# Loads moved to ScalarE's queue, five steps ahead, and the seeds of the last product moved up

## The chip, the cores and the metric

The kernel runs on one core of a Trainium2 chip. The core has five engines with instruction queues of their own: TensorE (PE, with its weight loads shown as PEld), VectorE (DVE), ScalarE (ACT), GpSimd (POOL) and SyncE (SP). SP, POOL and ACT can also issue DMA transfers, which sixteen DMA engines carry out. An engine takes its queue in order: an instruction that waits holds up all behind it. The metric is the device time of one execution in microseconds, the median over the runs of the kernel.

## The reference

One encoder layer on x of 1024 rows and 2048 columns, in float32:

```python
h = rmsnorm(x, pre_g) * (1.0 + scale) + shift            # scale, shift, gate from silu(c) @ w_ada + b_ada
q, k, v, gate_a, u, gate_p = jnp.split(h @ w_in, SPLIT_POINTS, axis=-1)
y_a = windowed_gqa(q, k, v, rel_table, sink) * silu(gate_a)   # window 128, relative bias, sink
y_p = multiscale_pool(u, w_pool_grp, pool_scale) * silu(gate_p)
g_a, g_p = jnp.split(sigmoid(h @ w_merge + b_merge), 2, axis=-1)
merged = g_a * (y_a @ w_branch_attn) + g_p * (y_p @ w_branch_pool)
return x + gate * rmsnorm(merged @ w_out, post_g)
```

## The kernel before, in words

**Products.** A float32 operand is split into a high and a low part (`split`, lines 90 to 92: ACT writes the high part, DVE subtracts for the low one), and a product is hi x hi, hi x lo and lo x hi. The large products run by a Strassen scheme with seven products instead of eight for each 2 x 2 of blocks, named B11, T3, T2, B21, T4, T1, B22. For `h @ [w_in, w_merge]` (`strassen`, line 198) the weights come in 34 pairs of 128 columns. A pair is seven products of 12 matmuls, one after another, into banks called X, Z and V. Its weights are loaded by SP (`raw`), summed by DVE, split by ACT and DVE into a ring of four (`whi`, `wlo`), and the banks are evicted by ACT. The inner dimension is taken in two halves: a first pass over all 34 pairs with the first 1024 columns of h (partial sums go to `part_d`), and a second pass with the others.

**Side work.** While PE multiplies, `run` (line 309) calls one step of a queue `side` at given points of each pair; with `every` of (0, 1, 3, 4, 6) these are five steps a pair. `placed` puts a step's PE and DVE instructions behind the last matmul and the last low-part split issued so far (`tc.issue_after`). Apart from such edges a planner sets the order on every engine: it takes the instructions that are ready by its own cost model's times, those written first going first, so work may be issued earlier than it is written, and a wait that lasts longer on the chip than in the model holds up what stands behind it.

**Bias lines** (`bias_lines`, line 594) run in the first pass as one side step: a small product gives one line of 512 relative-bias values per head; ACT evicts it, POOL stores it to `line_d` and then copies it 128 times for each of 8 heads into `bias_d` (2 MB, DRAM to DRAM), which attention reads much later.

**The x stage** (lines 687 to 752) is made of the last ten pairs of the first pass, 50 side steps. It builds the second half of h, transposed. `fetch_x` loads a tile of 128 x 512 of x through POOL's queue (`side_load`) and scales it on ACT; three steps later `turn_x` transposes it with four matmuls, and ACT copies the result into H. There are sixteen tiles, in a ring of four (`xt2`). Sixteen steps of `modulate` and four of `pre_op` follow. Into these steps `with_sums` hangs eight of the sixteen weight sums for the output product: `weight_sums` (line 628) loads four tiles of `w_out` through POOL into a ring of four of their own (`ws2`), DVE makes four sums three steps later, and POOL stores them to `ws_d`. They start at steps 2, 6, ..., 30. In the last pair, the planned operand of the second pass begins to be split (`refill`, line 741), and more of it follows in the first pair of the second pass.

**The end.** The output product runs in four blocks of seven products of 48 matmuls. `load_wo` fetches the weights of a product, `prep_wo` splits them, `product` (line 1109) multiplies and calls `prep_wo` for the next one. In the last block (lines 1319 to 1355) T4, T1 and B22 go row by row (`by_rows`), so that bank t is done after a quarter of the product. `squares` sums a result's squares on ACT, `weigh` multiplies it by the gate row on DVE, and `finish_rows` closes a row of 128 x 2048: the norm's factor, four operations on DVE (line 1316) and four stores by SP. B22 accumulates on top of seeds: DVE adds `last["12"]` to the banks that hold T1's result, after these were weighed. Before the change the four rows of the first half are closed in one loop behind T4, and the seeds of B22 follow behind T1.

Of the kernel before, what the change touches and what calls it, by code (L numbers as in the profile page):

```python
# [20 lines left out]
P = 128  # L21
# [21 lines left out]
def encoder_layer(ctx: ExitStack, tc: tile.TileContext, x, c, table, w_ada, b_ada, pre_g,  # L43
# [27 lines left out]
    dram = ctx.enter_context(tc.tile_pool(name="dram", bufs=1, space=DRAM))  # L71
    psum = ctx.enter_context(tc.tile_pool(name="psum", bufs=4, space=PSUM))

    cnt, pairs_, last_mm, last_lo = [0], [0], [None], [None]

    def uid(s):
        cnt[0] += 1
        return f"{s}_{cnt[0]}"

    def bank(tag, name="b"):  # L80
        return psum.tile([P, 512], F32, tag=tag, name=uid(name), bufs=1 if tag in SEEDED else 2)
# [6 lines left out]


    def split(hi, lo, src):  # L90
        nc.scalar.activation(hi, src, AF.Copy)  # L91
        return nc.vector.tensor_tensor(lo, src, f32(hi), ALU.subtract)  # L92

    def placed(f):
# [6 lines left out]
    def add(o, a, b, eng=None):  # L101
        (eng or nc.vector).tensor_tensor(o, a, b, ALU.add)  # L102
# [467 lines left out]
    def pass1(n, side, every=(0, 2, 4, 6), then=None):  # L570
        nonlocal i
        for m in range(n):
            w, n0 = weight_of(ORDER[i])
            run(strassen(w, n0, 0, range(4), op, to_dram(block(part_d, ORDER[i]))),
                side, every, None, then if m == n - 1 else None)
            i += 1
# [17 lines left out]
    def bias_lines():  # L594

        nc.gpsimd.memset(tab, 1.0)
        side_load(tab[0:32, :], table)
        oh = ev.tile([P, 512], F32, tag="ev", name="oh")[0:33, :]
        side_load(oh, onehot)
        pb = bank("sc")  # L600
        nc.tensor.matmul(pb[0:NH, :], tab, oh, start=True, stop=True)
        bl = ev.tile([P, 512], F32, tag="ev", name="bl")[0:NH, :]
        nc.scalar.activation(bl, pb[0:NH, :], AF.Copy)
        side_store(line_d, bl)
        side_store(bias_d.rearrange("h (p l) -> h p l", l=LINE),
              bass.AP(line_d.tensor, line_d.offset, [[LINE, NH], [0, P], [1, LINE]]))

    grow = gp.tile([KT, 4, P], F32, name="grow")
# [39 lines left out]
    def with_sums(steps, first, stride, ns, tile_):  # L648

        got = {}  # L650

        def begin(f, n):
            got[n] = weight_sums(n, tile_)
            f()

        def end(f, n):
            f()
            got.pop(n)()

        for i_, n in enumerate(ns):  # L660
            a, b = first + i_ * stride, first + i_ * stride + 3
            steps[a] = lambda f=steps[a], n=n: begin(f, n)
            steps[b] = lambda f=steps[b], n=n: end(f, n)
        return steps
# [25 lines left out]
    h = {HALF + k: [H[s][:, k] for s in range(2)] for k in range(HALF)}  # L690

    def x_tile():
        return sp.tile([P, 512], F32, tag="xt2", name=uid("xt"), bufs=4)

    def sum_tile():
        return sp.tile([P, 512], F32, tag="ws2", name=uid("wsum"), bufs=4)

    def fetch_x(si, q):
        xt = x_tile()
        c0 = 1024 + q * 512  # L700
        side_load(xt, x[si * P:(si + 1) * P, c0:c0 + 512])
        nc.scalar.activation(xt, xt, AF.Copy, scale=rstd[:, si:si + 1])
        return xt

    def turn_x(si, q, xt):
        pt = bank("sc")
        for j in range(4):
            nc.tensor.transpose(pt[:, j * P:(j + 1) * P], xt[:, j * P:(j + 1) * P], ident)
        nc.scalar.activation(H[si // 4][:, 4 * q:4 * q + 4, (si % 4) * P:(si % 4 + 1) * P],
                             pt.rearrange("p (k t) -> p k t", k=4), AF.Copy)  # L710

    held = {}

    def x_step(n):
        if n < 2 * NB:
            held[n] = fetch_x(n // 2, n % 2)
        if n >= 3:
            turn_x((n - 3) // 2, (n - 3) % 2, held.pop(n - 3))

    steps = [lambda n=n: x_step(n) for n in range(2 * NB + 3)]  # L720
    steps += [lambda k=k, s=s: modulate((nc.scalar, nc.vector)[s], h[k][s], k) for k in h for s in range(2)]
    side = deque(with_sums(steps, 2, 4, range(8, 16), sum_tile))
    h1, h2 = ({j: h[HALF + ktile(kh, j)] for j in range(4)} for kh in range(2))
    t2 = {}

    def pre(j):
        t2[j] = pre_op(j, h1, h2, x_tile)

    side.extend(lambda j=j: pre(j) for j in range(4))

    def put_all(o, name, h1, h2, t2):
        for j in range(4):
# [13 lines left out]
                                                             3: part_of("T1"), 5: part_of("B22")}  # L746

    op2, ahead, before, among = refill(h1, h2, t2)
    pass1(PAIRS - i, side, (0, 1, 3, 4, 6), ahead)
    assert not side  # L750
    all_of(before)
    op = op2
# [353 lines left out]
            ws.append((hi, lo))  # L1106
        ready.append(ws)

    def product(mov, banks, fresh, by_rows=False):
        ws = ready.popleft()  # L1110
        load_wo()
        order = [(t, j) for t in range(4) for j in range(KS)] if by_rows else \
            [(t, j) for j in range(KS) for t in range(4)]
        for t, j in order:
            hi, lo = op[mov][j]
            wh, wl = ws[j]
            ts_ = slice(t * P, (t + 1) * P)
            for n, (m_, w_) in enumerate(((hi, wh), (hi, wl), (lo, wh))):
                nc.tensor.matmul(banks[t], m_[:, ts_], w_, start=fresh and j == 0 and n == 0,  # L1119
                                 stop=j == KS - 1 and n == 2, skip_group_check=True)  # L1120
        prep_wo()

    def four(tag, bufs=4):
        return [ev.tile([P, 512], F32, tag=tag, name=uid(tag), bufs=bufs) for _ in range(4)]
# [177 lines left out]
    def fetch_rows(half, t):  # L1302
        si = half * 4 + t
        rows_x[si] = [slot("xr", F32) for _ in range(4)]
        for n in range(4):
            side_load(rows_x[si][n], x[si * P:(si + 1) * P, n * 512:(n + 1) * 512])

    def finish_rows(half, t):
        si = half * 4 + t
        s_ = const.tile([P, 4], F32, tag="st", name=uid("st"), bufs=2)  # L1310
        nc.vector.tensor_reduce(s_[:, 0:1], ssq[:, si], op=ALU.add, axis=AX.X)
        nc.scalar.activation(s_[:, 1:2], s_[:, 0:1], AF.Sqrt, bias=eps_t, scale=1.0 / D)
        nc.vector.reciprocal(s_[:, 2:3], s_[:, 1:2])
        for n in (1, 3, 2, 0):
            o_ = (last, kept)[n % 2][f"{n // 2 + 1}{half + 1}"][t]
            nc.vector.scalar_tensor_tensor(o_, o_, s_[:, 2:3], rows_x[si][n], op0=ALU.mult, op1=ALU.add)  # L1316
            store(out[si * P:(si + 1) * P, n * 512:(n + 1) * 512], o_)

    bx, bz = new_banks(3)
# [7 lines left out]
    for t in range(2):  # L1327
        fetch_rows(0, t)
    product("T3", bz, False)
    for t in range(4):  # L1330
        add(bx[t], bz[t], last["21"][t])
    for t in range(4):
# [1 line left out]
        sub(last["12"][t], last["12"][t], bz[t])  # L1334
    for t in range(2, 4):
        fetch_rows(0, t)
    product("T4", bx, False, by_rows=True)
    for t in range(2):
        fetch_rows(1, t)
    for t in range(4):  # L1340
        squares(0, "21", t, bx[t])
        weigh(0, "21", last["21"][t], bx[t])
        finish_rows(0, t)
    product("T1", bz, False, by_rows=True)
    for t in range(2, 4):
        fetch_rows(1, t)
    for t in range(4):
        squares(0, "22", t, bz[t])
        weigh(0, "22", last["22"][t], bz[t])
        add(bz[t], bz[t], last["12"][t])  # L1350
    product("B22", bz, False, by_rows=True)
    for t in range(4):
        squares(0, "12", t, bz[t])
# [40 lines left out]
```

## Time and profile before

| | |
|---|---|
| median of 3 runs | 2172.62 us (2171.68 to 2174.97) |
| profiled execution, its own time | 2174.68 us |
| its span, first to last instruction | 2172.8 us |
| mean granted clock of PE | 0.988 |
| PE busy | 2101.9 us, 97% |
| DVE busy | 1501.2 us, 69% |
| ACT busy | 1081.7 us, 50% |
| POOL busy | 187.7 us, 9% |
| first pass, x stage: loads of x issued | 555.4 to 635.1 us |
| last block: first matmul of B22 | 2147.98 us |

A line of the profile's timeline gives the start, the duration, the engine, the line of the kernel, the operation with the tile written and those read, the count, and in brackets the idle time of the engine before it and what ended it. Instructions that only issue a DMA are shown on SPq, ACTq or POOL. A line of the waits gives the total, the count and the longest. Matmuls are pipelined: PE shows 0.39 us for one of 512 columns, and the next one starts 0.23 us later.

### The profile page before, as it was taken

What the parts mean: (1) busy time and instruction counts of PE and PEld (TensorE: products, weight loads), DVE (VectorE), ACT (ScalarE), POOL (GpSimd) and SP (SyncE); (2) the same over time, 40 slices, a digit from 0 to 9 for tenths busy, and PEclk for the clock granted to TensorE, in tenths of its full rate; (3) what the DMA queues carried; (4) which work ended last, traced back from release to release, by engine and by line L of the source; (5) the groups of instructions that cost most, each with busy time, mean ns of one, the idle gap of its engine ahead of it and who ended that gap; (6) DMA issues with size and microseconds to landing.
All of it is one profiled execution on the core that took longest, in us unless ns stands there. A gap on an engine that the chain in (4) does not pass through costs nothing.

```text
span 2172.8 us, 29010 instructions
## 1 busy us (share of the span) xinstructions
PE 2101.9 (97%) x9638; PEld 1725.6 (79%) x9638; DVE 1501.2 (69%) x2695; ACT 1081.7 (50%) x2006; POOL 187.7 (9%) x407
## 2 busy tenths in 40 slices
PE   5999999889989999999999999999999999999997
PEld 3688788668878888888888888888788888788885
DVE  6688556777446686767776777866967987655558
ACT  6664444234364464576667433333645655545342
POOL 0402102431232000000000000000000000000021
PEclk9999999999999999999999999999999999999998
DMA  9768645997567446455554576675654646776367
GB/s 329 263 228 300 210 154 201 333 325 235 184 222 243 137 151 206 160 168 170 182 173 140 190 225 217 214 236 170 231 168 162 213 138 205 253 262 227 98 213 252
DMA packets 267430, 455.63 MB, mean 210 GB/s; under 512 B 24154, under 2 KB 120562, under 8 KB 267280
## 3 DMA queue, kind: packets, MB, share of 16 engines
q1 hardware_dynamic: 238048, 359.21, 50.5%
q0 software_dynamic: 28896, 94.51, 12.8%
q8 instruction: 76, 1.25, 0.2%
q14 instruction: 74, 0.61, 0.1%
q10 hardware_dynamic: 336, 0.06, 0.0%
HBM read 321.53 MB, written 134.24 MB: 210 GB/s over the span
## 4 chain that ended last, share of the span: by engine, by line
PE 78%; DMA 12%; DVE 6%; issue 2%; ACT 1%; POOL 1%; SPq 0%; DVEq 0%; ACTq 0%; POOLq 0%
PE Z L222 26%; PE V L222 18%; PE X L222 18%; PE OUT L1119 11%; DMA ada<-in_w_ada_dram 2%; DMA gada<-in_w_ada_dram 2%; DMA xt<-in_x_dram 1%; DMA raw<-in_w_merge_dram 1%; DVE wlo L92 1%; DMA raw<-in_w_in_dram 1%; DVE po L1316 1%; DMA gt<-proj_d 1%; PE PT L851 1%; DMA lm<-m_d 1%; PE GEMV L432 1%
## 5 line engine op out<-in xcount | busy, mean ns | idle before, releaser
L91 ACT ACTIVATE whi<-raw 128x512 fp32r<-128x512 f32 (+1 forms) x540 | 321.2, 600 | 512.6 <-PE Z L222 247.1
L92 DVE TENSOR_TENSOR wlo<-raw,whi 128x512 fp32r<-128x512 f32 (+1 forms) x540 | 347.6, 650 | 166.5 <-PE Z L222 107.1
L102 DVE TENSOR_TENSOR raw<-raw,raw 128x512 f32<-128x512 f32 x78 | 53.8, 690 | 122.9 <-DMA raw<-in_w_merge_dram 73.0
L92 DVE TENSOR_TENSOR wlo<-wr,whi 128x512 fp32r<-128x512 f32 x112 | 76.2, 687 | 76.9 <-ACT whi L91 74.9
L91 ACT ACTIVATE whi<-wr 128x512 fp32r<-128x512 f32 x112 | 69.3, 627 | 100.1 <-PE OUT L1119 98.2
L222 PE MATMUL X<-B11h,whi 128*128 128x512 f32 x336 | 94.3, 399 | 7.9 <-ACT c L292 5.4
L222 PE MATMUL V<-T3h,whi 128*128 128x512 f32 x336 | 93.4, 396 | 8.5 <-DVE u L102 7.8
L222 PE MATMUL V<-T4h,wlo 128*128 128x512 f32 x336 | 91.9, 393 | 1.9 <-DVE wlo L92 1.9
L222 PE MATMUL X<-B11l,whi 128*128 128x512 f32 x336 | 93.2, 396 | 0.4 <-DVE B11l L92 0.4
L222 PE MATMUL V<-T4h,whi 128*128 128x512 f32 x336 | 92.9, 395 | 0.5 <-ACT T4h L91 0.5
L222 PE MATMUL Z<-T2h,whi 128*128 128x512 f32 x336 | 91.9, 392 | 1.4 <-ACT Z L248 1.4
L222 PE MATMUL Z<-T2h,wlo 128*128 128x512 f32 x336 | 91.8, 392 | 1.4 <-DVE wlo L92 1.4
L222 PE MATMUL Z<-T1h,whi 128*128 128x512 f32 x336 | 92.4, 392 | 0.8 <-ACT T1h L91 0.7
L222 PE MATMUL X<-B11h,wlo 128*128 128x512 f32 x336 | 93.2, 397 | 0.0
L222 PE MATMUL Z<-B22h,whi 128*128 128x512 f32 x336 | 92.1, 393 | 0.6 <-ACT u L271 0.6
L222 PE MATMUL V<-T3l,whi 128*128 128x512 f32 x336 | 92.4, 394 | 0.0
L222 PE MATMUL V<-T3h,wlo 128*128 128x512 f32 x336 | 92.2, 394 | 0.0
L222 PE MATMUL X<-B21h,wlo 128*128 128x512 f32 x336 | 91.1, 390 | 1.1 <-DVE wlo L92 1.1
L222 PE MATMUL X<-B21h,whi 128*128 128x512 f32 x336 | 92.0, 392 | 0.0
L222 PE MATMUL V<-T4l,whi 128*128 128x512 f32 x336 | 91.9, 393 | 0.0
L222 PE MATMUL Z<-T2l,whi 128*128 128x512 f32 x336 | 91.5, 391 | 0.0
L222 PE MATMUL Z<-B22h,wlo 128*128 128x512 f32 x336 | 91.1, 390 | 0.0
(361 smaller groups left out, 5041.9 us busy)
## 6 DMA issues: line engine op xcount, KB each, us to landing
part<-part_d SPq DMA_DIRECT2D x136, 256.0 KB, 4.8
raw<-in_w_merge_dram SPq DMA_DIRECT2D x64, 512.0 KB, 5.5
raw<-in_w_in_dram SPq DMA_DIRECT2D x60, 512.0 KB, 4.1
ada<-in_w_ada_dram POOLq DMA_DIRECT2D x96, 256.0 KB, 6.0
proj_d<-part SPq DMA_DIRECT2D x68, 256.0 KB, 2.2
wsum<-in_w_out_dram POOLq DMA_DIRECT2D x64, 256.0 KB, 6.2
ws_d<-wsum POOLq DMA_DIRECT2D x64, 256.0 KB, 4.9
gada<-in_w_ada_dram POOLq DMA_DIRECT2D x32, 512.0 KB, 6.5
```

What stands on the lines that cost most here:

```text
L91: nc.scalar.activation(hi, src, AF.Copy)
L92: return nc.vector.tensor_tensor(lo, src, f32(hi), ALU.subtract)
L102: (eng or nc.vector).tensor_tensor(o, a, b, ALU.add)
L222: last_mm[0] = nc.tensor.matmul(ps, w_[:, i], op[mov][j][m_], start=fresh and i == 0 and n == 0, stop=i == nj - 1 and n == 2, skip_group_c ...
L432: nc.tensor.matmul(pv[g][r:r + 32, :], scz[:, kc, :], tiles[kc][:, g], start=b == 0, stop=b == 3, tile_position=(0, r))
L851: nc.tensor.transpose(pt[:, i * P:(i + 1) * P], p[:, i * P:(i + 1) * P], ident)
L1119: nc.tensor.matmul(banks[t], m_[:, ts_], w_, start=fresh and j == 0 and n == 0, stop=j == KS - 1 and n == 2, skip_group_check=True)
L1316: nc.vector.scalar_tensor_tensor(o_, o_, s_[:, 2:3], rows_x[si][n], op0=ALU.mult, op1=ALU.add)
```

## The change

1. The broadcast of the bias lines into `bias_d` is issued by ACT instead of POOL; the small store before it stays on POOL.
2. The loads of x in the x stage are issued by ACT. The ring `xt2` has eight tiles and serves the weight sums too (`ws2` is gone; the memory is the same). A tile is turned five steps after its load, not three. The scaling on ACT moves from the load to the turn and is put behind the newest high-part split (`last_hi`).
3. The stage's eight weight sums start at steps 17, 21, ..., 45 instead of 2, 6, ..., 30, and the queue of steps is filled up to 50 with empty ones.
4. In the last block, T1's weights are split behind T3 (an extra `prep_wo`), and T4 splits none; B22's weights are split behind the closing of rows 0 and 1 of the first half (on DVE, behind its last operation, `last_lo`). Row 2 is closed behind T1's matmuls, and row 3 behind the seed of B22's first bank.

```diff
     def split(hi, lo, src):
-        nc.scalar.activation(hi, src, AF.Copy)
+        last_hi[0] = nc.scalar.activation(hi, src, AF.Copy)
         return nc.vector.tensor_tensor(lo, src, f32(hi), ALU.subtract)
...
-        side_store(bias_d.rearrange("h (p l) -> h p l", l=LINE),
+        nc.scalar.dma_start(bias_d.rearrange("h (p l) -> h p l", l=LINE),
...
     def x_tile():
-        return sp.tile([P, 512], F32, tag="xt2", name=uid("xt"), bufs=4)
-
-    def sum_tile():
-        return sp.tile([P, 512], F32, tag="ws2", name=uid("wsum"), bufs=4)
+        return sp.tile([P, 512], F32, tag="xt2", name=uid("xt"), bufs=8)
 
     def fetch_x(si, q):
         xt = x_tile()
         c0 = 1024 + q * 512
-        side_load(xt, x[si * P:(si + 1) * P, c0:c0 + 512])
-        nc.scalar.activation(xt, xt, AF.Copy, scale=rstd[:, si:si + 1])
+        nc.scalar.dma_start(xt, x[si * P:(si + 1) * P, c0:c0 + 512])
         return xt
 
     def turn_x(si, q, xt):
+        with tc.issue_after(last_hi[0].ins):
+            nc.scalar.activation(xt, xt, AF.Copy, scale=rstd[:, si:si + 1])
         pt = bank("sc")
...
-    held = {}
+    held, AHEAD = {}, 5
...
-        if n >= 3:
-            turn_x((n - 3) // 2, (n - 3) % 2, held.pop(n - 3))
+        if n >= AHEAD:
+            turn_x((n - AHEAD) // 2, n % 2 ^ AHEAD % 2, held.pop(n - AHEAD))
...
-    side = deque(with_sums(steps, 2, 4, range(8, 16), sum_tile))
...
-    side.extend(lambda j=j: pre(j) for j in range(4))
+    steps += [lambda j=j: pre(j) for j in range(4)]
+    every = (0, 1, 3, 4, 6)
+    steps += [lambda: None] * (len(every) * (PAIRS - i) - len(steps))
+    side = deque(with_sums(steps, 2 * NB + 1, 4, range(8, 16), x_tile))
...
-            nc.vector.scalar_tensor_tensor(o_, o_, s_[:, 2:3], rows_x[si][n], op0=ALU.mult, op1=ALU.add)
+            last_lo[0] = nc.vector.scalar_tensor_tensor(o_, o_, s_[:, 2:3], rows_x[si][n],
+                                                        op0=ALU.mult, op1=ALU.add)
...
     product("T3", bz, False)
+    prep_wo()
...
-    product("T4", bx, False, by_rows=True)
+    product("T4", bx, False, by_rows=True, prepare=False)
     for t in range(2):
         fetch_rows(1, t)
-    for t in range(4):
+
+    def close_rows(t):
         squares(0, "21", t, bx[t])
         weigh(0, "21", last["21"][t], bx[t])
         finish_rows(0, t)
+
+    for t in range(2):
+        close_rows(t)
+    with tc.issue_after(last_lo[0].ins):
+        prep_wo()
     product("T1", bz, False, by_rows=True)
     for t in range(2, 4):
         fetch_rows(1, t)
+    close_rows(2)
     for t in range(4):
         squares(0, "22", t, bz[t])
         weigh(0, "22", last["22"][t], bz[t])
         add(bz[t], bz[t], last["12"][t])
+        if t == 0:
+            close_rows(3)
```

More of the change, by code (lines that the diff above doesn't have):

```diff
@@ L72, in encoder_layer @@
     psum = ctx.enter_context(tc.tile_pool(name="psum", bufs=4, space=PSUM))
-    cnt, pairs_, last_mm, last_lo = [0], [0], [None], [None]
+    cnt, pairs_, last_mm, last_lo, last_hi = [0], [0], [None], [None], [None]
     def uid(s):
@@ L716, in x_step @@
             held[n] = fetch_x(n // 2, n % 2)
-        if n >= 3:
-            turn_x((n - 3) // 2, (n - 3) % 2, held.pop(n - 3))
-    steps = [lambda n=n: x_step(n) for n in range(2 * NB + 3)]
+        if n >= AHEAD:
+            turn_x((n - AHEAD) // 2, n % 2 ^ AHEAD % 2, held.pop(n - AHEAD))
+    steps = [lambda n=n: x_step(n) for n in range(2 * NB + AHEAD)]
     steps += [lambda k=k, s=s: modulate((nc.scalar, nc.vector)[s], h[k][s], k) for k in h for s in range(2)]
-    side = deque(with_sums(steps, 2, 4, range(8, 16), sum_tile))
     h1, h2 = ({j: h[HALF + ktile(kh, j)] for j in range(4)} for kh in range(2))
@@ L748, in encoder_layer @@
     op2, ahead, before, among = refill(h1, h2, t2)
-    pass1(PAIRS - i, side, (0, 1, 3, 4, 6), ahead)
+    pass1(PAIRS - i, side, every, ahead)
     assert not side
@@ L1107, in prep_wo, with product @@
         ready.append(ws)
-    def product(mov, banks, fresh, by_rows=False):
+    def product(mov, banks, fresh, by_rows=False, prepare=True):
         ws = ready.popleft()
@@ L1120, in product @@
                                  stop=j == KS - 1 and n == 2, skip_group_check=True)
-        prep_wo()
+        if prepare:
+            prep_wo()
     def four(tag, bufs=4):
@@ L1343, in encoder_layer @@
         finish_rows(0, t)
+    for t in range(2):
+        close_rows(t)
+    with tc.issue_after(last_lo[0].ins):
+        prep_wo()
     product("T1", bz, False, by_rows=True)
```

## The prediction

> **What bounds the kernel now.** I read the page first, then the busy time of the engines over stretches of 50 us to find where TensorE (PE) idles, then those places in order of time.
>
> ```profile
> span 2172.8 us, 29010 instructions
> PE 2101.9 (97%) x9638; PEld 1725.6 (79%) x9638; DVE 1501.2 (69%) x2695; ACT 1081.7 (50%) x2006; POOL 187.7 (9%) x407
> ```
>
> PE is busy for 2101.9 us of 2172.8, so an edit that removes none of its matmuls can win only from its idle time and from stretches at a low granted clock. The change touches three places. The largest is the stage that loads the second half of x. Below are the busy times over its first four pairs of weight columns (each stretch runs from one pair's B11 to the next), one clean pair behind them, all four together, and, in the second fence, only the transposes in the first of them. Columns: stretch, us, then PE, PEld, DVE, ACT and POOL busy, granted clock, DMA share, GB/s.
>
> ```profile
> 569.28:589.17 19.89, 19.89 (x94) 16.46 (x92) 10.95 (x17) 10.31 (x18) 4.58 (x9) 1.00 0.71 228
> 589.17:611.64 22.47, 21.71 (x107) 17.64 (x106) 10.53 (x16) 10.78 (x20) 6.88 (x13) 1.00 0.71 235
> 611.64:639.19 27.55, 22.31 (x108) 17.51 (x106) 11.04 (x17) 18.91 (x33) 8.67 (x17) 0.99 0.74 246
> 639.19:663.09 23.90, 23.90 (x100) 19.54 (x101) 14.59 (x23) 13.13 (x23) 7.03 (x13) 0.87 0.65 221
> 663.09:682.13 19.04, 19.04 (x85) 15.77 (x84) 11.98 (x20) 8.01 (x13) 4.85 (x9) 1.00 0.79 240
> 569.28:663.09 93.81, 87.81 (x401) 71.16 (x400) 47.11 (x73) 53.13 (x92) 27.16 (x51) 0.96 0.70 233
> ```
>
> ```profile
> 569.28:589.17 19.89, 0.95 (x8) 0.98 (x8) 1.00 0.71 228
> ```
>
> A clean pair takes 19.04 us. The first stretch holds eight transposes, that is two groups of four, and takes 19.89 us, so a group costs PE (19.89 - 19.04) / 2 = 0.42 us. All sixteen groups fall in the four pairs. They should last 4 x 19.04 + 16 x 0.42 = 82.9 us and last 93.81: **10.9 us are lost**. Most of it is one stall:
>
> ```profile
> 624.76 0.54 POOL L701 DMA_DIRECT2D xt<-in_x_dram  x1
> 630.83 0.54 POOL L635 DMA_DIRECT2D wsum<-in_w_out_dram  x1 [2.79 <-DMA ws_d<-wsum]
> 631.36 1.06 POOL L701 DMA_DIRECT2D xt<-in_x_dram  x2
> 637.93 0.72 ACT L702 ACTIVATE xt<-xt,rstd 128x512 f32<-128x512 f32 x1 [5.21 <-DMA xt<-in_x_dram]
> 638.56 0.58 ACT L292 ACTIVATE c<-X 128x512 f32<-128x512 f32 x1
> 639.19 2.07 PE L222 MATMUL X<-B11h,whi 128*128 128x512 f32 x4 [4.66 <-ACT c L292]
> ```
>
> ```profile
> 639.19:644.47 5.28, 5.28 (x12) 4.01 (x13) 3.28 (x5) 4.29 (x8) 0.80 (x2) 0.50 0.67 220
> ```
>
> ```profile
> ACT xt L702 <- DMA xt<-in_x_dram: 23.2, 6, 6.1
> ```
>
> To be seen: on POOL's queue the x load stands behind a weight-sum load that waits 2.79 us for a store; ScalarE (ACT) reaches the scaling of that x tile and waits 5.21 us for it; the eviction of bank X stands behind the scaling, and PE, which needs the bank, stands 4.66 us. Then it runs twelve matmuls at a granted clock of 0.50 in 5.28 us, where a clean pair takes 19.04 / 7 = 2.72: another 2.6 us. So one such block costs 4.66 + 2.6 = **7.3 us**. ACT waited for x six times, 23.2 us in all.
>
> The second place is the end. Here VectorE (DVE) is the bound:
>
> ```profile
> 2133.00:2169.30 36.30, 24.56 (x95) 19.46 (x94) 32.50 (x62) 9.57 (x28) 6.29 (x12) 0.84 0.90 325
> ```
>
> ```profile
> DVE po L1262 <- ACT jk L1259: 2.8, 1, 2.8
> ```
>
> ```profile
> L1316 DVE SCALAR_TENSOR_TENSOR po<-po,st,xr 128x512 f32<-128x512 f32 x32 | 21.9, 745 | 0.1
> ```
>
> ```profile
> 2143.90 2.73 DVE L1316 SCALAR_TENSOR_TENSOR po<-po,st,xr 128x512 f32<-128x512 f32 x4
> 2147.98 0.77 PE L1119 MATMUL OUT<-whi,B22h 128*128 128x512 f32 x1 [4.35 <-DVE OUT L102]
> 2166.49 2.74 DVE L1316 SCALAR_TENSOR_TENSOR po<-po,st,xr 128x512 f32<-128x512 f32 x4
> ```
>
> PE waits 4.35 us for the seeds of the last product, which stand in DVE's queue behind the closing of row 3 of the first half. But DVE itself is busy for 32.50 of 36.30 us, up to its last instruction at 2166.49 + 2.74 = 2169.2; the 3.6 us behind it are the last store. Only its 3.8 us of idle time can go, and 2.8 of them are one wait, for the last product's first row. PE's wait is worth what it takes out of that.
>
> **The change part by part.** (1) *x through ACT's queue, five steps ahead.* Sixteen loads leave POOL, and no weight sum runs on POOL while they are fetched. ACT gains sixteen issues. The nearest rows are ACT's own loads at the start and the x loads as they are now:
>
> ```profile
> L340 ACTq DMA_DIRECT2D rows<-in_pre_norm_g_dram x1: 442/442/442, 2.1 to 2.1; - x1
> DMA to landing us min/median/max: 3.4/5.0/8.1
> ```
>
> 16 x 0.44 = 7.1 us of ACT, which is busy 53.13 of the 93.81 us; it lies beside PE's matmuls. If that cover were gone it would cost at most these 7.1. A pair has five steps, so a step is at least 19.04 / 5 = 3.8 us, and a load issued five steps ahead has 19 us to land where the slowest took 8.1. The scaling now stands at the turning step, behind the newest high-part split, so what ACT waited for is long there; evictions no longer stand behind it. The new wait, of a load for the tile freed eight loads earlier, ends three steps ahead of the load (tile k - 8 is turned at step k - 3). Queued behind such a load on ACT would be evictions and splits, which PE waits for (the slower rival). Ends: all 10.9 us won, or one block of 7.3 left and 3.6 won. I take all but 2.6: twice the 1.3 us that the second pair loses without any long stall (22.47 - 19.04 - 5 x 0.42), since nothing shows that a newly planned order has fewer small waits than that. **Won: 8.3.**
>
> The Trainium skill, page "DMA: Bandwidth & Descriptors", section "Issuing engines are not separate DMA queues", says that transfers from ScalarE, SyncE and GpSimd run on the same 16 DMA engines and interleave, so that another issuing engine saves only issue time. By that rule alone the move to ACT would win nothing here. The rows show POOL's order (2.79 us behind a store) at work, and the lookahead is a second edit; but with a DMA share of 0.70 the rule is the ground of the third rival.
>
> (2) *Weight sums later.* Their 32 loads, 32 stores and 32 VectorE operations move from steps 2 to 33 to steps 17 to 48, of 50. The steps up to 44 fall where DVE has room: 11.98 of 19.04 us above, sums included. The last sum lands in the last pair, where DVE fills the next operand:
>
> ```profile
> 760.00:800.00 40.00, 40.00 (x179) 33.11 (x177) 39.24 (x65) 29.32 (x54) 0.00 (x0) 1.00 0.40 138
> 792.94 0.68 DVE L92 TENSOR_TENSOR T1l<-H,T1h 128x512 fp32r<-128x512 f32 x1
> 794.56 1.07 PE L222 MATMUL Z<-T1l,whi 128*128 128x512 f32 x4
> ```
>
> DVE is full there (39.24 of 40). T1's last low part is done at 793.6 and read at 794.56, a slack of 0.9 us. Four more operations of 0.68 are 2.7 us, so between 0 and 1.8 us of PE are lost; I take the middle, **0.9 lost**.
>
> (3) *Bias lines.* Only the 2 MB broadcast moves; its small source still leaves on POOL.
>
> ```profile
> 239.26 0.52 POOL L604 DMA_DIRECT2D line_d<-bl  x1 [1.50 <-ACT bl L603]
> 241.12 0.60 ACT L292 ACTIVATE c<-X 128x512 f32<-128x512 f32 x1 [0.29 <-PE X L222]
> 243.10 1.10 POOL L605 DMA_DIRECT2D bias_d<-line_d  x1 [2.23 <-DMA line_d<-bl]
> 246.37 1.07 PE L222 MATMUL X<-B11h,whi 128*128 128x512 f32 x4
> 258.95 0.69 DVE L102 TENSOR_TENSOR raw<-raw,raw 128x512 f32<-128x512 f32 x1 [11.02 <-DMA raw<-in_w_in_dram]
> 260.30 1.19 PE L222 MATMUL X<-B21h,wlo 128*128 128x512 f32 x4 [1.07 <-DVE wlo L92]
> ```
>
> ACT would wait for the same landing, at most from 239.26 to 243.10, 3.8 us, and issue for up to 1.10. Behind it stands the eviction of X, done at 241.72 and needed at 246.37: 4.65 us of cover, so at worst 4.9 - 4.65 = 0.3 is lost. The broadcast still delays the weight load that cost PE 1.07 us; if it got out of the way, 1.1 would be won. I take **0**.
>
> (4) *The end.* T1's weights are split one product earlier, from tiles already there; the last product's weights wait behind row 1's closing on DVE, and rows 2 and 3 close later, row 3 behind the first seed. No operation is added. Row 3's closing (four operations, 2.73 us) can now fill the 2.8 us in which DVE waited for the last product's first row. Ends: 0 (the work behind only shifts) and 3.8 (all of DVE's idle time); **2.8 won**, the one long wait, since nothing else of DVE's idle time is addressed.
>
> Sum: 8.3 - 0.9 + 0 + 2.8 = **10.2 us**. The profiled execution took 2174.68 us by the clock of the runs (span 2172.8, 1.9 around it), 2.1 above the median of 2172.62; its sum is 2164.5. The same off the median: **2162.4**.
>
> **The rivals.** *One block stays.* The planner places ACT's instructions by its own times, so an eviction can still stand behind something late once. For it: ACT's whole order is planned anew. Against: six waits had one cause. Then 3.6 - 0.9 + 2.8 = 5.5: 2167.1.
>
> *Transfers are late whoever issues them.* If sharing of the DMA engines (share 0.70) makes x late, the new queue changes nothing in the stage, and the end alone gains 2.8 - 0.9 = 1.9: 2170.7. Against: landings of 8.1 at most fit in 19 us.
>
> *ACT is blocked by its own loads (slower).* A load on ACT waits for the tile of k - 8; if PE runs behind the planner's times, everything behind the load on ACT waits too, evictions first. Price: 7.3 us a block, as above. Without any small wait left the gain would be 10.2 + 2.6 = 12.8; one or two blocks (7.3, 14.6) leave a gain or about nothing, and from the third on the kernel is slower: 3 x 7.3 - 12.8 = 9.1, 2181.7. For it: eight of the loads have such a wait, and ACT has no other way around. Against: the tile is freed three steps, some 11 us, earlier.
>
> **How the numbers follow.** A measurement of this kernel can tell about 0.2%, 4.3 us, from no change. The forecast has 0.55, one block 0.17 (0.12 of it beyond 4.3 us, 0.05 within), late transfers 0.13, the blocked queue 0.10, and 0.05 is for a larger gain than the sum's parts, because the whole order is planned again. Faster: 0.55 + 0.12 + 0.05 = 0.72; the same: 0.05 + 0.13 = 0.18; slower: 0.10. Range: the best ends, 10.9 + 3.8 + 1.1 = 15.8, give 2156.8; the worst end without a blocked queue, 3.6 - 1.8 - 0.3 + 0 = 1.5, gives 2171.1. I take 2157 to 2171, which leaves the blocked queue out. The forecast alone lies within 2158 to 2167.
>
> **What would show it.** Right: ACT's wait for x falls from 23.2 us to under 3; the four pairs of the x loads last 83 to 87 us with the clock at 1.00; PE's wait for the last product falls under 3 us, while the time from 2133 to the last DVE operation shrinks only by about 3. Wrong: a wait of an ACT-issued load for PE, a gap of PE in the last of these ten pairs over 1.8 us, or a new gap near the bias broadcast. A total beyond 2171 would say that ACT's queue is the new bound.

## The result, and the profile after

The changed kernel takes 2146.22 us (median; 2139.41 to 2147.93) against 2172.57 before: a ratio of 0.9871, 95% interval 0.9847 to 0.9895. That is 26 us faster, where 10.2 were forecast, and it lies below the range of 2157 to 2171. The profiled execution took 2147.93 us.

The head of the page of the changed kernel:

```profile
span 2146.1 us, 28998 instructions
...
PE 2090.2 (97%) x9638; PEld 1717.2 (80%) x9638; DVE 1499.2 (70%) x2695; ACT 1084.1 (51%) x2006; POOL 178.2 (8%) x390
```

PE's busy time fell by 11.7 us although it does the same 9638 matmuls: some ran at a low granted clock before. The other 15 us of the span's 26.7 were idle time of PE.

To find the places, I set the same instructions of both traces side by side: the bias matmul (line 601), the first gate-column matmul (614), the first scores of attention, the last B11, the end. First the kernel before, then the changed one (min/median/max in ns, then the first and the last start in us):

```profile
L601 PE MATMUL b<-oh,tab x2: 586/587/588, 237.3 to 237.8; 33*8 33x512 f32 x2
L614 PE MATMUL b<-ones,gacc x32: 164/250/354, 543.3 to 547.1; 128*128 128x1 f32 x32
```

```profile
L601 PE MATMUL b<-oh,tab x2: 586/586/587, 239.6 to 240.0; 33*8 33x512 f32 x2
L614 PE MATMUL b<-ones,gacc x32: 165/250/251, 524.1 to 527.5; 128*128 128x1 f32 x32
```

Between these two marks lie 543.3 - 237.3 = 306.0 us before and 524.1 - 239.6 = 284.5 after: **21.5 us of the 26.7 were won in the stage behind the bias lines**, which the prediction had at zero. The rest by the same marks: 2.3 lost ahead of the bias matmul, 4.8 won from the gate columns to the first scores (859.0 to 835.0), 2.1 given back in the middle, and 4.8 won from the last B11 on (84.5 to 79.7). The 2.3 are mostly one wait of PE for a small load: the bias matmul waits 3.02 us for the load of its operand `oh` in the changed kernel, and not at all in the run of the bias line alone below, so they aren't put down to the change.

**Where the 21.5 us were.** Busy times over the stretches of that stage (us, then PE, PEld, DVE, ACT and POOL busy, granted clock, DMA share, GB/s), before and after:

```profile
285.00:350.00 65.00, 65.00 (x289) 53.83 (x288) 32.25 (x49) 27.69 (x45) 0.00 (x0) 1.00 0.39 131
350.00:400.00 50.00, 45.47 (x207) 36.96 (x206) 37.63 (x49) 18.37 (x30) 26.05 (x49) 1.00 0.90 306
400.00:450.00 50.00, 45.02 (x187) 37.29 (x186) 39.12 (x53) 16.00 (x27) 16.68 (x32) 0.90 0.97 342
450.00:500.00 50.00, 42.86 (x178) 33.93 (x177) 35.78 (x48) 15.68 (x28) 14.39 (x27) 0.97 0.90 305
```

```profile
285.00:350.00 65.00, 65.00 (x289) 53.84 (x288) 46.69 (x65) 27.14 (x44) 24.54 (x46) 1.00 0.85 284
350.00:400.00 50.00, 50.00 (x230) 41.71 (x229) 37.57 (x55) 20.53 (x34) 11.77 (x22) 1.00 0.83 278
400.00:450.00 50.00, 50.00 (x222) 41.40 (x222) 35.15 (x49) 20.69 (x34) 11.72 (x22) 1.00 0.88 290
450.00:500.00 50.00, 48.25 (x213) 39.66 (x212) 35.87 (x50) 20.44 (x34) 11.79 (x22) 1.00 0.84 272
```

Before, POOL does nothing from 285 to 350 us and the DMA share is 0.39. From 350 to 500 the work that was put off comes all at once: a DMA share of 0.90 to 0.97, and PE busy for only 133.35 of 150 us. After, the share is 0.83 to 0.88 throughout, and PE loses 1.75 us. POOL's row and the two rows of DVE that belong to it (timeline, before):

```profile
351.00 1.06 POOL L455 DMA_DIRECT2D ada<-in_w_ada_dram  x2 [68.57 <-DVE acc L459]
...
263.16 1.28 DVE L459 SCALAR_TENSOR_TENSOR acc<-ada,sc,acc 128x1024 f32<-128x1024 f32 x1
349.42 1.28 DVE L459 SCALAR_TENSOR_TENSOR acc<-ada,sc,acc 128x1024 f32<-128x1024 f32 x1
```

POOL waits 68.57 us for a tile that an accumulation of the modulation (line 459) frees. That accumulation runs at 349.42 with no idle time ahead of it: DVE came to it only then, 86 us after the one before, though it was busy for just 32.25 of the 65 us from 285 to 350. So what was late was neither DVE's time nor a transfer, but the accumulation's place in DVE's order. After, the accumulations of the same line per stretch read (DVE busy for this line alone, us and count; before in the first fence):

```profile
285.00:350.00 65.00, 0.58 (x1) 1.00 0.39 131
350.00:400.00 50.00, 17.37 (x14) 1.00 0.90 306
```

```profile
285.00:350.00 65.00, 16.05 (x13) 1.00 0.85 284
350.00:400.00 50.00, 1.29 (x1) 1.00 0.83 278
```

**The x stage.** The four pairs that turn x, and then the last pair of the pass with the first two of the next, changed kernel; behind them the same last three before:

```profile
567.47:651.31 83.84, 83.84 (x401) 69.35 (x400) 40.90 (x63) 52.52 (x90) 12.97 (x24) 1.00 0.61 189
...
727.47:747.57 20.10, 19.34 (x85) 15.70 (x84) 14.92 (x25) 12.48 (x22) 2.17 (x4) 1.00 0.44 153
747.57:769.52 21.95, 19.28 (x75) 14.31 (x74) 21.01 (x36) 13.62 (x25) 0.00 (x0) 0.93 0.47 167
769.52:791.33 21.81, 21.81 (x97) 18.02 (x95) 16.80 (x28) 8.97 (x16) 0.00 (x0) 0.99 0.53 175
```

```profile
758.29:777.33 19.04, 19.04 (x85) 15.77 (x84) 17.89 (x30) 14.36 (x27) 0.00 (x0) 1.00 0.32 106
777.33:796.37 19.04, 19.04 (x85) 15.77 (x84) 19.01 (x32) 13.55 (x25) 0.00 (x0) 1.00 0.47 160
796.37:815.41 19.04, 19.04 (x85) 15.77 (x84) 13.43 (x22) 6.77 (x11) 0.00 (x0) 1.00 0.58 198
```

The x pairs went from 93.81 us to 83.84, with PE busy all the time: 10.0 won. But those three late pairs went from 57.12 to 63.86 us: **6.7 of it lost again**.

**The end.** From the last B11 to the first matmul of B22, and from there to DVE's last operation, before and after:

```profile
2088.30:2147.98 59.68, 55.34 (x244) 45.38 (x243) 42.95 (x76) 23.82 (x53) 18.09 (x34) 0.99 0.70 240
2147.98:2169.23 21.25, 13.93 (x48) 10.97 (x48) 17.58 (x34) 3.91 (x12) 0.00 (x0) 0.74 0.88 316
```

```profile
2066.40:2121.49 55.09, 55.09 (x244) 45.63 (x243) 39.12 (x68) 23.33 (x50) 17.11 (x33) 1.00 0.71 237
2121.49:2142.56 21.07, 11.34 (x49) 8.75 (x47) 21.03 (x42) 4.80 (x15) 0.95 (x2) 0.83 1.00 381
```

PE's wait of 4.35 us is gone, the first part is 4.6 us shorter, and the second is as long as it was: DVE, busy for 17.58 of 21.25 us there before, is now busy for 21.03 of 21.07.

### The profile page after: what moved, and what is told of

Read it like the earlier page. It is cut to its first block, busy times and chain, and to the rows that moved or that the text cites. A ratio compares the mean times of both kernels' runs of the same rounds, so it can differ in the third digit from the quotient of the medians.

```text
span 2146.1 us, 28998 instructions
## 1 busy us (share of the span) xinstructions
PE 2090.2 (97%) x9638; PEld 1717.2 (80%) x9638; DVE 1499.2 (70%) x2695; ACT 1084.1 (51%) x2006; POOL 178.2 (8%) x390
## 4 chain that ended last, share of the span: by engine, by line
PE 80%; DMA 11%; DVE 7%; issue 2%; ACT 1%; SPq 0%; DVEq 0%; POOL 0%; ACTq 0%; POOLq 0%
PE Z L222 26%; PE V L222 18%; PE X L222 18%; PE OUT L1119 11%; DMA raw<-in_w_merge_dram 2%; DVE wlo L92 2%; DMA ada<-in_w_ada_dram 1%; DMA raw<-in_w_in_dram 1%; DMA xt<-in_x_dram 1%; PE PT L851 1%; DMA xr<-in_x_dram 1%; DMA gt<-proj_d 1%; DMA lm<-m_d 1%; PE PV L862 0%; DMA raw<-in_w_branch_attn_dram 0%
## 5 line engine op out<-in xcount | busy, mean ns | idle before, releaser
L222 PE MATMUL X<-B21l,whi 128*128 128x512 f32 x336 | 92.2, 393 | 0.8 <-DVE B21l L92 0.8
L222 PE MATMUL Z<-T1l,whi 128*128 128x512 f32 x336 | 91.3, 390 | 0.0
```

Source lines behind the costliest of these rows:

```text
L222: last_mm[0] = nc.tensor.matmul(ps, w_[:, i], op[mov][j][m_], start=fresh and i == 0 and n == 0, stop=i == nj - 1 and n == 2, skip_group_c ...
```

## The experiments

All ratios are against runs of the kernel before on the same chip, taken beside them. In the table: from the bias matmul to the gate columns; the four x pairs; the three late pairs, that is the last of the first pass and the first two of the second (57.12 when nothing is lost); from the last B11 to the end of the span. Pairs are measured between the first matmuls of their B11.

| kernel | median us | ratio, 95% interval | bias to gate | x pairs | late pairs | last B11 to end |
|---|---|---|---|---|---|---|
| before | 2172 to 2174 | 1 | 306.0 | 93.81 | 57.12 | 84.5 |
| changed | 2146.22 | 0.9871 (0.9847 to 0.9895) | 284.5 | 83.84 | 63.86 | 79.7 |
| bias line alone | 2148.16 | 0.9893 (0.9873 to 0.9913) | 281.0 | 92.71 | 57.12 | 83.6 |
| changed, bias line undone | 2165.7 | 0.9972 (0.9959 to 0.9985) | 305.7 | 83.84 | 64.28 | 79.7 |
| x stage alone | 2171.1 | 0.9995 (0.998 to 1.0009) | 306.0 | 83.84 | 65.51 | 84.2 |
| end alone | 2169.81 | 0.9988 (0.9975 to 1.0002) | 301.7 | 93.92 | 57.12 | 79.8 |

### One part at a time

The bias line alone on the kernel before:

```diff
-        side_store(bias_d.rearrange("h (p l) -> h p l", l=LINE),
+        nc.scalar.dma_start(bias_d.rearrange("h (p l) -> h p l", l=LINE),
```

> The kernel before with one line changed: the 2 MB broadcast of the bias lines is issued by ACT. Theory A (the whole unexpected gain comes from this line, since the order of DVE and POOL behind it is planned anew: the two traces' marks differ by 21.5 us between the bias matmul and the gate columns): 18 to 22 us faster. Theory B (the gain comes from the edits of the x stage and of the end, and the marks only shift): within 3 us of before. The step of the prediction gave 0, from 0.3 lost to 1.1 won.

Measured: 0.9893, that is 23.2 us faster (0.0107 x 2172). Theory A holds: this one line is worth nearly the whole gain. The stage behind it takes 281.0 us, and PE is busy for 279.8 of them; from 400 to 500 us, where it had lost most before, without a break:

```profile
400.00:450.00 50.00, 50.00 (x222) 41.42 (x221) 33.97 (x47) 21.00 (x35) 10.12 (x19) 1.00 0.85 287
450.00:500.00 50.00, 50.00 (x221) 41.10 (x221) 38.70 (x54) 20.35 (x33) 11.79 (x22) 1.00 0.80 273
```

The reverse, the changed kernel with that line undone:

```diff
-        nc.scalar.dma_start(bias_d.rearrange("h (p l) -> h p l", l=LINE),
+        side_store(bias_d.rearrange("h (p l) -> h p l", l=LINE),
```

> The changed kernel with the broadcast back on POOL. Theory A: the gain falls from 26 to about 5 to 8 us. Theory B: it stays above 22 us. The prediction's sum without step (3) is 10.2 us.

Measured: 0.9972, 6.1 us faster than before. The other edits together are worth about 6, not 10.2.

The x stage's edits alone (the second and third part of the change, nothing else):

> The kernel before with the x stage's edits alone (loads on ACT, five ahead, later weight sums). The prediction's steps (1) and (2): 8.3 - 0.9 = 7.4 us faster. By the two traces' marks from the end of the first stage to the first scores of attention: 4.8 us. If sharing of the DMA engines sets the x loads: 0.

Measured: 0.9995, no difference that can be told. In the table its x pairs win the 10.0 us, and its late pairs lose 8.4 (65.51 - 57.12). So the mechanism that was forecast is there, and nearly all of its gain is given back 60 us later.

The end alone (the fourth part, nothing else):

> The kernel before with the reordering of the end alone. The prediction's step (4): 2.8 us faster, 3.8 at most if only DVE's idle time can go. By the two traces' marks behind the last B11: 4.8 us.

Measured: 0.9988, 2.6 us, with an interval that reaches from 5.4 us faster to 0.4 slower. The traces say it more sharply: from the last B11 to the end, the three kernels in the table with the old end and a good or bad start alike (before, bias line alone, x stage alone) show 83.6 to 84.5 us, the three with the new end 79.7 to 79.8. So it is worth 3.8 to 4.8 us. (One trace alone has its scatter: this run leaves the stage from the bias matmul to the gate columns as it was, and shows 301.7 us there against 306.0.)

### The bias line: the order, or the transfer?

The broadcast could be dear on the chip because POOL's queue carries 2 MB, or because of what the planner puts behind it. Two kernels tell them apart. In the first it stays on POOL, behind the last load of the stage:

```diff
+    last_gp = [None]
...
-        side_load(at, w_ada[kc * P:(kc + 1) * P, 2 * D + q * 1024:2 * D + (q + 1) * 1024])
+        last_gp[0] = side_load(at, w_ada[kc * P:(kc + 1) * P, 2 * D + q * 1024:2 * D + (q + 1) * 1024])
...
-        side_store(bias_d.rearrange("h (p l) -> h p l", l=LINE),
-              bass.AP(line_d.tensor, line_d.offset, [[LINE, NH], [0, P], [1, LINE]]))
+    def spread_lines():
+        with tc.issue_after(last_gp[0].ins):
+            side_store(bias_d.rearrange("h (p l) -> h p l", l=LINE),
+                  bass.AP(line_d.tensor, line_d.offset, [[LINE, NH], [0, P], [1, LINE]]))
...
-    side.extend((gate_columns, gate_row))
+    side.extend((gate_columns, lambda: (gate_row(), spread_lines())))
```

> The kernel before with the broadcast of the bias lines still issued by POOL, but put behind the last load of the gate stage in POOL's queue (one edge of order). DVE's order behind it is then that of the version with ACT. Theory A (the place of the broadcast in POOL's order, and the late accumulations planned behind it, cost the 23 us; not the transfer and not the queue that carries it): 19 to 24 us faster than before, 2148 to 2153. Theory B (a 2 MB transfer through POOL's queue is dear on the chip wherever it stands): less than 8 us faster.

Measured: 0.9989 (0.9975 to 1.0003), no gain: by the numbers Theory A as I had put it falls, and Theory B would do. The trace says something else. The stage behind the bias lines takes 288.5 us, so its gain of 17.5 us is there. It is lost in the next stage (POOL's timeline, then busy times):

```profile
491.75 1.11 POOL L610 DMA_DIRECT2D bias_d<-line_d  x1
...
606.58 1.21 POOL L706 DMA_DIRECT2D xt<-in_x_dram  x2 [55.27 <-PE b L713]
```

```profile
600.00:650.00 50.00, 41.62 (x192) 32.36 (x191) 22.61 (x36) 32.41 (x56) 19.36 (x36) 0.93 0.83 261
650.00:700.00 50.00, 42.86 (x180) 34.01 (x179) 28.30 (x47) 18.84 (x32) 17.32 (x32) 0.93 0.72 235
```

POOL issues the broadcast in 1.11 us and then, behind it, stands 55.27 us with the x loads, for tiles that transposes free which now stand late in PE's order (the first of them starts at 605.37 with no wait). From 600 on the loads come bunched, and PE idles 15.5 of 100 us. It is the same picture one stage later, now with other loads behind the broadcast. The second kernel decides: the same place, an eighth of the transfer.

```diff
-        side_store(bias_d.rearrange("h (p l) -> h p l", l=LINE),
-              bass.AP(line_d.tensor, line_d.offset, [[LINE, NH], [0, P], [1, LINE]]))
+        side_store(bias_d[0:1].rearrange("h (p l) -> h p l", l=LINE),
+              bass.AP(line_d.tensor, line_d.offset, [[LINE, 1], [0, P], [1, LINE]]))
...
-                    load(bt[e], bass.AP(bias_d.tensor, bias_d[h].offset + 127, [[LINE - 1, P], [1, SPAN]]))
+                    load(bt[e], bass.AP(bias_d.tensor, bias_d[0].offset + 127, [[LINE - 1, P], [1, SPAN]]))
```

> The kernel before with the broadcast cut to its first head: POOL copies 128 rows of 2 KB (256 KB) instead of 1024 rows (2 MB), and attention reads this one bias for all heads (the other seven are left out). On PE, DVE, ACT and SP every instruction stands in the same order as before, and on POOL too. Theory A (the order is what costs: loads and accumulations planned late behind a POOL broadcast, whatever it moves): within 3 us of before, and POOL still stands idle some 68 us for an accumulation. Theory B (the 2 MB transfer through POOL's queue is what costs on the chip): at least 15 us faster.

Measured: 0.9982 (0.9966 to 0.9997), 3.9 us at the middle of the interval, where Theory B wanted 15 and Theory A under 3. The broadcast's line before, and then the same of this kernel, POOL's next long wait in its timeline, and two of its stretches:

```profile
L605 POOL DMA_DIRECT2D bias_d<-line_d x1: 1098/1098/1098, 243.1 to 243.1; - x1
...
DMA to landing us min/median/max: 16.7/16.7/16.7
```

```profile
L605 POOL DMA_DIRECT2D bias_d<-line_d x1: 552/552/552, 243.4 to 243.4; - x1
...
DMA to landing us min/median/max: 3.7/3.7/3.7
```

```profile
349.74 1.06 POOL L455 DMA_DIRECT2D ada<-in_w_ada_dram  x2 [74.16 <-DVE acc L459]
```

```profile
400.00:450.00 50.00, 44.19 (x184) 36.63 (x183) 39.81 (x53) 15.91 (x26) 16.92 (x33) 0.90 0.96 334
450.00:500.00 50.00, 43.13 (x187) 34.39 (x186) 35.59 (x48) 16.49 (x29) 14.07 (x27) 1.00 0.89 305
```

The transfer lands in 3.7 us instead of 16.7 and holds POOL for half as long, and still POOL waits 74.16 us for an accumulation and PE loses as much from 400 to 500 (12.7 us idle, 12.1 before). So some 19 of the 23 us hang on the order, and about 4 (by the interval 0.7 to 7.4) on the transfer. What in the planner's costs makes a broadcast on POOL push back what stands behind it, whether it moves 256 KB or 2 MB, isn't settled by these runs.

### The x stage: which edit won, and which lost

Four variants of the changed kernel (all with the bias line on ACT and the new end), and one without some of its work:

| kernel | median us | ratio, 95% interval | bias to gate | x pairs | late pairs |
|---|---|---|---|---|---|
| changed: x on ACT, 5 ahead, sums late | 2146.22 | 0.9871 (0.9847 to 0.9895) | 284.5 | 83.84 | 63.86 |
| x on POOL, 5 ahead, sums late | 2141.41 | 0.9852 (0.9834 to 0.9871) | 281.5 | 83.84 | 61.01 |
| x on POOL, 3 ahead, sums late | 2139.82 | 0.9843 (0.9821 to 0.9865) | 282.4 | 83.84 | 62.77 |
| x on ACT, 5 ahead, sums closer | 2141.68 | 0.9852 (0.9832 to 0.9872) | 281.1 | 83.84 | 57.12 |
| x on ACT, 3 ahead, sums early | 2135.14 | 0.9823 (0.9804 to 0.9842) | 285.7 | 86.42 | 57.12 |
| changed, three sums without DVE work | 2137.55 | 0.9846 (0.9821 to 0.9872) | 284.4 | 83.84 | 58.11 |

(In the row with the sums early the turns reach into a fifth pair: 105.46 us for the five, less one clean pair of 19.04.) By the times only the version with the sums early stands clear of the changed kernel, and barely; the intervals of the others overlap with its own, so what an edit does is read from the traces here.

x on POOL again, five steps ahead:

```diff
-        nc.scalar.dma_start(xt, x[si * P:(si + 1) * P, c0:c0 + 512])
+        side_load(xt, x[si * P:(si + 1) * P, c0:c0 + 512])
```

> The changed kernel with the loads of x back on POOL's queue, still five steps ahead and with the sums late. If the lookahead and the absence of sums on POOL make the gain: the four pairs of the x loads stay at 84 us and the time within 2 us of the changed kernel. If ACT's queue makes it: up to 10 us slower than the changed kernel, with ACT waiting for x. By the rule that the issuing engine saves only issue time: the same.

Measured: the x pairs stay at 83.84 us and the time is not above the changed kernel's. ACT's queue is not what won. The Trainium skill, page "DMA: Bandwidth & Descriptors", section "Issuing engines are not separate DMA queues", says just that: the issuing engine saves issue time only. Here the trace agrees, 83.84 us by either queue.

And three steps ahead on POOL, as it is written before the change:

```diff
-        nc.scalar.dma_start(xt, x[si * P:(si + 1) * P, c0:c0 + 512])
+        side_load(xt, x[si * P:(si + 1) * P, c0:c0 + 512])
...
-    held, AHEAD = {}, 5
+    held, AHEAD = {}, 3
```

> The changed kernel with x loaded by POOL, three steps ahead as before; what stays of the x stage's edits are the late sums, the shared ring and the scaling at the turn. If the sums between the x loads on POOL were the cause of the stall in the x pairs: the x pairs stay at 84 to 86 us and the time at 2141, as with five steps on POOL. If three steps are too few on POOL: ACT waits for x again and the x pairs go to 88 us or more.

Measured: 83.84 us again, with PE busy throughout and no wait of ACT for x among its waits:

```profile
541.57:625.41 83.84, 83.84 (x401) 69.35 (x400) 37.72 (x57) 53.19 (x92) 14.28 (x27) 1.00 0.62 182
```

So neither ACT's queue nor the five written steps are needed. But this run doesn't show that lookahead is of no use, since the loads do not run three steps ahead in it:

```profile
539.79 3.77 POOL L698 DMA_DIRECT2D xt<-in_x_dram  x7 [11.37 <-DMA part_d<-c]
```

The planner places the loads as early as the shared ring of eight tiles allows, seven at once here. From the ninth tile on a tile is turned 32.6 to 35.3 us after its load was issued, as with five steps on POOL; before the change it was 12.3 to 22.1 from the fifth tile on. So late sums, a larger ring and the scaling at the turn are left, and no run has one of them alone. Apart from the empty steps, the one edit of this stage that stands in every version without the long stall, whatever its queue, ring and sums, is the scaling at the turn.

Now the loss behind. Sums closer together, so that the last two pairs are free:

```diff
-    side = deque(with_sums(steps, 2 * NB + 1, 4, range(8, 16), x_tile))
+    side = deque(with_sums(steps, 2 * NB, 3, range(8, 16), x_tile))
```

> The changed kernel with the eight weight sums of the x stage started at steps 16, 19, ..., 37 (three apart instead of four), so that the last one ends at step 40 and the last two pairs have none but that. Theory A (the late sums cost what the x stage gains: from the pair behind the x loads to the first scores 183.7 us against 176.9 before): 5 to 7 us faster than the changed kernel, about 2140. Theory B (the loss comes from the shared ring or the new order, not from the sums' place): the same as the changed kernel. Against both: three steps apart the transfers are denser, and if weight loads come late the gain goes again.

Measured: 4.5 us below the changed kernel by the medians, with intervals that overlap, and the late pairs at 57.12. But it is the warning in the expectation that came true: three pairs in the middle of the sums take 20.59, 21.03 and 23.48 us (65.10 for 57.12), and DVE waits for weight loads, 21.4 us in four times between 640 and 740 us:

```profile
DVE raw L102 <- DMA raw<-in_w_merge_dram: 21.4, 4, 7.7
```

The stage is no better than in the changed kernel. What the median gained lies elsewhere, 3.4 us of it in the stage behind the bias lines, which varies from 281.0 to 288.5 us among the kernels with the good order.

What is late in the late pairs? The last three sums keep their transfers, and lose their DVE operations:

```diff
+            if n < 13:
-            sub(a21, a11, a21)
-            sub(a22, a22, a21)
-            add(a11, a11, a22)
-            sub(a12, a12, a22)
+                sub(a21, a11, a21)
+                sub(a22, a22, a21)
+                add(a11, a11, a22)
+                sub(a12, a12, a22)
...
```

> The changed kernel with the four VectorE operations of each of the last three weight sums of the x stage left out; their loads and stores stay (the tiles are stored as loaded). The changed kernel loses 6.7 us in the last two pairs of the stage and the first of the second pass (63.86 us for the three, 57.12 before). If DVE's extra operations are what is late there: these three pairs return to 57 to 59 us. If the transfers of the sums are (DVE waits 4.5 us there for a weight load issued behind them): they stay at 61 us or more.

(The three pairs are those of the table, one pair later than the text of the expectation has them.)

Measured: the three pairs take 58.11 us, 5.75 less than in the changed kernel. By the condition as I had put it that is DVE's operations. The traces don't bear it out. The changed kernel:

```profile
720.10 0.68 DVE L105 TENSOR_TENSOR xt<-xt,xt 128x512 f32<-128x512 f32 x1
...
723.47 1.13 POOL L635 DMA_DIRECT2D xt<-in_w_out_dram  x2 [1.84 <-DMA ws_d<-xt]
724.90 1.20 POOL L635 DMA_DIRECT2D xt<-in_w_out_dram  x2 [0.30 <-issue]
...
729.47 0.69 DVE L92 TENSOR_TENSOR B11l<-H,B11h 128x512 fp32r<-128x512 f32 x1 [0.43 <-PE X L222]
734.64 0.69 DVE L102 TENSOR_TENSOR raw<-raw,raw 128x512 f32<-128x512 f32 x1 [4.47 <-DMA raw<-in_w_in_dram]
...
741.26 0.69 DVE L102 TENSOR_TENSOR xt<-xt,xt 128x512 f32<-128x512 f32 x1
...
743.81 1.20 PE L222 MATMUL V<-T4h,wlo 128*128 128x512 f32 x4 [0.76 <-DVE wlo L92]
```

Eight of the twelve operations are done by 720.8 us, before the first split of the new operand at 729.47; only the last sum's four stand among the splits, 0.60 us apiece. What DVE waits 4.47 us for is a weight load issued at 726.3, right behind the last sum's four loads, and landed 8.3 us later; before the change the same load landed in 4.2 and DVE waited 0.41. By an estimate from these rows, 4.06 us more of waiting and 4 x 0.60 of operations make 6.5 of the 6.74 us, as DVE then has hardly a pause for 30 us. The run without the operations changed both: its last sum is loaded from 708.92 us on, some 15 us earlier in its pairs, and the weight load lands in 4.7. So it doesn't separate operations from transfers, and that the four loads made the weight load late is argued, not shown. In five versions with the sums at these places this wait of DVE lasts 3.16 to 7.47 us and the late pairs lose 3.9 to 8.4; the version with the shortest wait loses least, and the one with the longest most.

Last, the sums back at their early steps, in a ring of their own, with x on ACT three steps ahead:

```diff
     def x_tile():
-        return sp.tile([P, 512], F32, tag="xt2", name=uid("xt"), bufs=8)
+        return sp.tile([P, 512], F32, tag="xt2", name=uid("xt"), bufs=4)
+
+    def sum_tile():
+        return sp.tile([P, 512], F32, tag="ws2", name=uid("wsum"), bufs=4)
...
-    held, AHEAD = {}, 5
+    held, AHEAD = {}, 3
...
-    side = deque(with_sums(steps, 2 * NB + 1, 4, range(8, 16), x_tile))
+    side = deque(with_sums(steps, 2, 4, range(8, 16), sum_tile))
```

> The changed kernel with x on ACT but three steps ahead, in a ring of four, and the sums at their old steps in their old ring. If the queue alone makes the gain of the x stage: four pairs of 84 us, and without the late sums 5 to 7 us faster than the changed kernel, about 2140. If the lookahead is needed: the pairs go back towards 93 us, and the time is that of the changed kernel or up to 4 us more.

Measured: 2135.14 us, ratio 0.9823 (0.9804 to 0.9842), **the lowest median here**: 37 us under the kernel before, and its interval lies just below the changed kernel's. ACT still waits for x:

```profile
ACT xt L706 <- DMA xt<-in_x_dram: 14.6, 6, 4.4
```

But these waits cost PE little now: the x pairs lose 2.6 us, not 10. And most of the 2.6 is not x at all but one gap of 1.92, behind DVE, which waits 6.93 us for a weight load:

```profile
611.93 0.69 DVE L105 TENSOR_TENSOR ws<-raw 128x512 f32<-128x512 f32 x1 [6.93 <-DMA raw<-in_w_merge_dram]
...
613.28 1.20 PE L222 MATMUL V<-T3h,whi 128*128 128x512 f32 x4 [1.92 <-DVE u L102]
```

Steps, ring and sums are as before the change here, so the long stall went by ACT's queue or by the scaling's place at the turn. Which of the two, I did not separate.

Turned four steps after the load instead of three, the turn written ahead of the load:

```diff
-    held, AHEAD = {}, 3
+    held, AHEAD = {}, 4
...
-        if n < 2 * NB:
-            held[n] = fetch_x(n // 2, n % 2)
         if n >= AHEAD:
             turn_x((n - AHEAD) // 2, n % 2 ^ AHEAD % 2, held.pop(n - AHEAD))
+        if n < 2 * NB:
+            held[n] = fetch_x(n // 2, n % 2)
```

> The version with x on ACT, a ring of four and the sums at their old steps (2135.1 us), with each tile turned four steps after its load instead of three (the turn stands ahead of the load in its step). If what it still loses in the x pairs (2.6 us, ACT waiting up to 4.4 us for x) is a lack of lookahead: 1 to 3 us faster, 2132 to 2134. If the loads are held by the ring of four: the same.

Measured: 2137.78 us, 0.982 (0.9797 to 0.9843): the same, as far as an interval of 10 us can tell. In the trace the x pairs lose 2.0 us instead of 2.6 (85.86) and ACT waits 12.7 us for x instead of 14.6. A fourth step does little; a larger ring with the early sums was not tried.

## Why the prediction was wrong

The sign was right; the size was not, since the step "(3) bias lines: I take 0" failed. It priced the broadcast by its own path: the wait for the landing, the issue, the eviction behind it, the weight load it delays, between 0.3 lost and 1.1 won. On the chip that path stayed about as cheap: PE's longest gap just behind the broadcast is 1.20 us, where it was 1.07. The order planned behind the broadcast was left out, and that was 23.2 us by the run of the line alone (21.5 by the marks). The trace of before held the clue: POOL idle for 68.57 us right behind, with a DMA share of 0.39 and then 0.97, and PE losing 16.7 us from 350 to 500. I read PE's idle time only where the change touches the code, and the waits of POOL as those of an engine that is not the bound. The case "a larger gain, because the whole order is planned again" had 0.05.

Step (1) got the size and not the cause. The x pairs won 10.0 us where 8.3 were taken; the first stall went, ACT's wait for x fell from 23.2 us to none, and the pairs took 83.84 us, inside the "83 to 87". Since they then lose nothing, a group of transposes costs (83.84 - 4 x 19.04) / 16 = 0.48 us and not 0.42. To which of its edits the gain belongs stays open. ACT's queue is not needed while the sums are late, and the five written steps are not either, though the ring of eight tiles keeps the loads as far ahead without them. The late sums are not needed for most of it: with the sums early 7.4 of the 10.0 us are won, by ACT's queue or by the scaling at the turn. I had named both the absence of the sums and the scaling's new place, and gave neither a number.

Step (2) was mis-sized: 0.9 lost (0 to 1.8) against 6.7. I counted four operations of the last sum against a slack of 0.9 us, and only those four did fall among the splits. What I left out is the moved transfers: the weight load behind the last sum's loads landed in 8.3 us instead of 4.2, and DVE waited 4.47 us for it instead of 0.41 (read from the traces; no run has the transfers without the operations in the same place). The bound took the trace of before, in which that load comes in time.

Step (4) was right in mechanism and too small: 2.8 taken, 3.8 as the end, about 4.6 measured (3.8 to 4.8 among the kernels). DVE's idle time from 2133 on was not the limit: with the order new, rows 0 and 1 are closed ahead of it, and B22's own stretch fills up from 17.58 to 21.03 us of DVE.

The sum by what was measured: 21.5 + 10.0 - 6.7 + 4.6 = 29.4 us, of which 26.7 arrive in the span. The marks show 2.3 lost ahead of the bias matmul and 2.1 in attention and the output product, and 1.5 more won from the gate columns to the scores and 0.2 behind the last B11 than these parts have; I can't tell them from the scatter between runs.

Of the rivals, the blocked ACT queue did not come: no wait of an eviction behind a load on ACT in this stage. "Transfers are late whoever issues them" has a part of the truth: with the sums early, ACT still waits 14.6 us for x by its own queue.

## What to carry to other kernels

Where a planner orders the engines, price an edit of one DMA twice: on the chip, and in the order of everything that stands behind it in the queue that it leaves. Look for an engine that stands idle for tens of us waiting for an instruction that starts without any wait of its own: there the order is late, not the data. And work that is moved out of one full place needs a sum over the place it goes to, its transfers included: here the late pairs lost two thirds of what the x pairs had won, and by the traces most of that to one weight load that landed late behind the moved loads.

## What I had not expected of the hardware

Little was the hardware's. Issuing a load of 128 x 512 of x held ACT for 0.33 us, where I had counted 0.44, and POOL for 0.54. And a transfer eight times smaller, landed in 3.7 us instead of 16.7, moved the time of the kernel by 0.2%, although the DMA share was above 0.9 soon after: its bytes were not what came together there. A weight load can be late at a moderate share too: the one that landed in 8.3 us instead of 4.2, right behind four side loads, did so at a DMA share of 0.62.

```profile
570.89 0.33 ACTq L698 DMA_DIRECT2D xt<-in_x_dram  x1
```
